# Two-layer hybrid encoder on one core: low parts of the queries two heads to a tile, second logits matmul over 64 rows

## The chip, the cores and the metric

The kernel runs on one core of a Trainium2 chip. The metric is the device time of one execution in microseconds (us). TensorE is called PE below, VectorE DVE, ScalarE ACT, GpSimd POOL; SP issues most DMA transfers.

## What is computed

Two layers of an encoder trunk on 512 tokens of width 1024. Each layer is a half-step FFN, a mixer of three branches, and another half-step FFN. The change lies in the mixer's two attention branches, which share one routine:

```python
# branch A: own chunk + 8 chunks to the left, learned relative bias; branch C: forgetting attention
qf = rms_norm(q, gq) * (dh ** -0.5)          # per head, 8 heads of 64
kf = rms_norm(k, gk)
logits = einsum('qhd,khd->hqk', qf, kf) + bias_or_forget_term      # masked
p = softmax(logits)
out = einsum('hqk,khd->qhd', p, v)
```

All inputs and outputs are f32.

## The kernel before

Matrix products are made from split operands: a number x is held as a rounded part `hi` (fp32r, the type that PE multiplies in one pass) and a rest `lo = x - hi`. A product of two split operands takes three matmuls (`triple`, L119 to L121): hi by hi, lo by hi, hi by lo.

Layout: the hidden state is transposed, features on the 128 partitions, 512 tokens in the columns. The eight heads of 64 are handled as four pairs p; a pair fills 128 partitions.

Queries and keys are projected with tokens on partitions, normalised, and then turned by PE, one pair at a time, into an "mm" bank of PSUM (`turn(p)`, L664). From there they go to blocks [128, 2, 512] of the pool "b", which has 17 blocks:

- Block `b` of a pair has one half for each head (`odd` = 0, 1). Half `odd` holds the head's 64 rows of hi in the rows `own` (0 to 63 for the first head, 64 to 127 for the second). In the rows `other` a key block holds the key's lo part (`low`, L679), and a query block holds the query's hi once more (L676).
- So the first logits matmul (L771), over all 128 rows, gives q_hi k_hi + q_hi k_lo at once.
- The term q_lo k_hi is left. For it each pair of queries has a second block, `lows[p]`: half `odd` has the head's lo in the rows `own` and zeros, written by a memset on POOL (L677), in the rows `other`. The second logits matmul (L772) runs over all 128 rows and adds this product to the same bank; the zeros meet the keys' lo.

`logits(h, i, strips)` makes one row block i (128 queries, (i + 1) x 128 keys) of head h: two matmuls, then DVE adds bias or mask and takes the maximum (L775), ACT the exponential (L779), POOL or, for i = 3, DVE scales (L782). `turn` of the attention transposes the probabilities on PE (L794) and splits them (L798, L799); `weigh` multiplies with the values (L816, L817) and brings the result out (L820, L821). There are 8 heads x 4 blocks in each branch, so 32 pairs of logits matmuls a branch and 128 in all.

Between these steps a filler feeds PE: branch A's attention is filled with the projections of branch C (among them the turning of C's queries once heads 2 and 4 of A are reached), branch C's with products of the merge. The Python code calls steps by delays counted in PE work (`later`, `poll`); the scheduler that builds the program then sets each engine's final order by its own estimate of times, so an edit of one step can move its neighbours.

Of the kernel before, what the change touches and what calls it, by code (L numbers as in the profile page):

```python
# [15 lines left out]
F32 = mybir.dt.float32  # L16
# [6 lines left out]
P = 128  # L23
# [7 lines left out]
HD = 64  # L31
# [9 lines left out]
def encoder_kernel(tc, xT, c, w_ada, b_ada, gains, w_gate, w_up, w_down, w_qkv, w_f, w_ubg,  # L41
                   qk_gain, rel, fbias, w_pool, pool_scale, w_branch, w_out, inv_cnt, w_first, out):
    nc = tc.nc
# [12 lines left out]
    mm = nc.tensor.matmul  # L56
# [7 lines left out]
    def st(shape, dt, tag, bufs):  # L64
        return sb.tile(shape, dt, tag=tag, bufs=bufs, name=nm(tag))
# [4 lines left out]
    def mmt(shape=(P, T)):  # L70
        return ps.tile(list(shape), F32, tag="mm", bufs=4, name=nm("mm"))

    def blk(tag, dt=F32R):
        bufs = {"xv": 4, "v2": 4, "b": NB}[tag]
        return st([P, 2, T], dt, tag, bufs)

    def t1(cols=T):
        return st([P, cols], F32, "t1", 2)

    def t2(cols=T):  # L80
        return st([P, cols], F32, "t2", 3)
# [16 lines left out]
    def later(delay, fn, group=None):  # L98
        t = Task(pe[0] + delay, fn, group)
        tasks.append(t)  # L100
        return t
# [267 lines left out]
    def split_to(hi, lo, src, lo_eng=nc.vector):  # L369
        nc.scalar.copy(hi, src)  # L370
        lo_eng.tensor_tensor(lo, src, hi.bitcast(F32), op=ALU.subtract)  # L371
# [266 lines left out]
    def proj_qk(l, col, gcol, is_q, res, pre=None, norm=None):  # L638
        lows = []
        qs = []  # L640

        def evac(t, a):
            if t == 0:
                qs.extend((st([P, NT, T], F32, "ptb", 2), st([P, NT, H], F32, "qss", 1)))
            qn, ss = qs
            nc.scalar.copy(qn[:, t, :], a)
            sq = t2(T)
            nc.scalar.activation(sq, a, AF.Square)  # L648
            nc.vector.tensor_reduce(ss[:, t, :], sq.rearrange("p (h d) -> p h d", h=H), axis=AX.X, op=ALU.add)

        yield from proj(l, col, evac, pre, norm)
        qn, ss = qs
        v = st([P, NT * H], F32, "nt_v32", 2)
        nc.vector.tensor_scalar(v, ss.rearrange("p t h -> p (t h)"), 1.0 / HD, EPS, op0=ALU.mult, op1=ALU.add)
        r = rsqrt(v, NT * H)
        for t in range(NT):
            q3 = qn[:, t, :].rearrange("p (h d) -> p h d", h=H)
            eng = nc.vector if t % 2 else nc.gpsimd
            eng.tensor_tensor(q3, q3, r[:, t * H:(t + 1) * H].unsqueeze(2).to_broadcast([P, H, HD]), op=ALU.mult)

        def turn(p):
            pt = mmt()
            for t in range(NT):
                nc.tensor.transpose(pt[:, t * P:(t + 1) * P], qn[:, t, p * P:(p + 1) * P], ident)  # L664
            pe[0] += 2.2
            b = blk("b")
            if is_q:
                lows.append(blk("b"))
            first, second = slice(0, HD), slice(HD, P)
            for odd, (own, other) in enumerate(((first, second), (second, first))):  # L670
                dst = b[:, odd, :]
                gc = gcol[own, :]
                nc.scalar.activation(dst[own, :], pt[own, :], AF.Identity, scale=gc)
                low = dst[other, :]
                if is_q:
                    nc.scalar.activation(low, pt[own, :], AF.Identity, scale=gc)  # L676
                    nc.gpsimd.memset(lows[p][other, odd, :].bitcast(F32), 0.0)  # L677
                    low = lows[p][own, odd, :]
                nc.vector.scalar_tensor_tensor(low, pt[own, :], gc, dst[own, :].bitcast(F32),  # L679
                                               op0=ALU.mult, op1=ALU.subtract)  # L680
            res.append((b, lows[p]) if is_q else b)

        todo = [lambda p=p: turn(p) for p in range(4)]
        turns.append(todo)

        def ready(p):
            if len(todo) >= 4 - p:
                if heads[0] < (Q_GATE if is_q else K_GATE)[p]:
                    later(8, lambda: ready(p))
                else:  # L690
                    while len(todo) >= 4 - p:
                        todo.pop(0)()

        for p in range(4):
            later(TURN + 12 * p, lambda p=p: ready(p))
# [6 lines left out]
    def finish_turns(upto=3):  # L702

        for todo in turns:
            while len(todo) >= 4 - upto:
                todo.pop(0)()
# [53 lines left out]
    def attention(qs, ks, vs, strip, ys, filler, budget, group):  # L760


        open_pt = {}

        def logits(h, i, strips):
            p, off = divmod(h, 2)
            (q, ql), k = qs[p], ks[p]
            odd = h % 2
            n = (i + 1) * P
            s = mmt()  # L770
            mm(s[:, :n], q[:, odd, i * P:(i + 1) * P], k[:, odd, :n], start=True, stop=False)  # L771
            mm(s[:, :n], ql[:, odd, i * P:(i + 1) * P], k[:, odd, :n], start=False, stop=True)  # L772
            lg = t1(T)[:, :n]
            mx = st([P, 1], F32, "mx", 4)
            nc.vector.tensor_tensor_reduce(out=lg, in0=s[:, :n], in1=strips[i], scale=-1.0, scalar=BIG,  # L775
                                           op0=ALU.add, op1=ALU.min, accum_out=mx)
            pr = t2(T)[:, :n]
            sm = st([P, 1], F32, "sm", 4)
            nc.scalar.activation(pr, lg, AF.Exp, bias=mx, scale=-1.0, accum_out=sm)  # L779
            rs = st([P, 1], F32, "rs", 4)  # L780
            nc.vector.reciprocal(rs, sm)
            (nc.vector if i == NT - 1 else nc.gpsimd).tensor_scalar(pr, pr, rs, None, op0=ALU.mult)  # L782
            pe[0] += 0.5 * (i + 1.5)
            later(LAG_T, lambda: turn(h, i, pr), group)

        def turn(h, i, pr):
            half, c = divmod(i, 2)
            nj = 2 * half + 2
            if c == 0:
                open_pt[h] = st([P, 2, nj, 256], F32R, "ptb" if half else "pta", 2 if half else 1)  # L790
            pt = open_pt[h]
            tp = mmt()
            for j in range(i + 1):
                nc.tensor.transpose(tp[:, j * P:(j + 1) * P], pr[:, j * P:(j + 1) * P], ident)  # L794
            tv = tp[:, :(i + 1) * P].rearrange("p (j q) -> p j q", q=P)
            dh = pt[:, 0, :i + 1, c * P:(c + 1) * P]
            dl = pt[:, 1, :i + 1, c * P:(c + 1) * P]
            nc.scalar.copy(dh, tv)  # L798
            nc.vector.tensor_tensor(dl, tv, dh.bitcast(F32), op=ALU.subtract)  # L799
            pe[0] += 0.55 * (i + 1)  # L800
            if c == 1:
                later(LAG_V, lambda: weigh(h, half, pt), group)

        def weigh(h, half, pt):
            p, off = divmod(h, 2)
            rows = slice(off * HD, off * HD + HD)
            other = slice(HD - off * HD, 2 * HD - off * HD)
            if off == 0 and half == 0:
                ys.append(blk("b"))
            y = ys[p]  # L810
            o = mmt((P, HALF))
            nj = 2 * half + 2
            for j in range(nj):
                q0 = P if j == nj - 1 else 0
                v2 = vs[j][:, h, :, :].rearrange("p a d -> p (a d)")
                mm(o[:, q0:], v2, pt[:, 0, j, q0:], start=(j == 0), stop=False)  # L816
                mm(o[:, q0:], v2, pt[:, 1, j, q0:], start=False, stop=(j == nj - 1))  # L817
            cols = slice(half * HALF, (half + 1) * HALF)
            yl = t1(T)[:, :HALF]
            nc.scalar.copy(yl[rows, :], o[other, :])  # L820
            nc.vector.tensor_tensor(yl[rows, :], o[rows, :], yl[rows, :], op=ALU.add)  # L821
            split_to(y[rows, 0, cols], y[rows, 1, cols], yl[rows, :], nc.gpsimd)
            pe[0] += 1.0 * nj

        for h in range(H):
            strips = strip(h)
            if group == "c":
                finish_turns(h // 2)
            for i in range(NT):
                logits(h, i, strips)  # L830
                if i == NT - 1:
                    heads[0] = h + 1
                poll()
                goal = pe[0] + budget
                while filler is not None and pe[0] < goal:
                    if next(filler, "end") == "end":
                        filler = None
                poll()
        if filler is not None:
            for _ in filler:  # L840
                pass
# [249 lines left out]
```

## Time and profile before

| what | value |
|---|---|
| median of 3 runs | 2472.27 us (2471.41 to 2472.57) |
| profiled execution, its own time | 2472.68 us |
| span in the profile | 2470.9 us |
| PE busy | 2424.9 us, 98% of the span |
| DVE, ACT, POOL busy | 1328.2, 981.6, 377.3 us |
| attention of A and C, layer 0 | about 459 to 685 us of the span |
| attention of A and C, layer 1 | about 1680 to 1908 us of the span |

The span runs from the first to the last instruction; the execution's own time has 1.8 us more around it. Matmuls are pipelined: a row of the timeline gives a start and a modelled duration, and the spacing of the starts tells what a matmul costs in a stream. L numbers are lines of the kernel before. In the changed kernel L673 and L676 become L674 and L677, L679 and L771 keep their numbers, and what follows L771 stands one line lower (L772 becomes L773, L794 L795).

### The profile page before, as it was taken

Reading aid. Unit: us, or ns where it says so; the run is one execution under the profiler, and the core shown is the slowest. Engines: PE = TensorE matmul, PEld = TensorE weight load, DVE = VectorE, ACT = ScalarE, POOL = GpSimd, SP = SyncE. Lnnn points to the kernel's source line nnn. Section 1 sums busy time; section 2 is a strip of 40 time slices with the busy share of each in tenths; the row PEclk is TensorE's granted clock in tenths of the full one; section 3 lists DMA queues with packets and bytes.
Section 4 is the critical chain, followed back from the end, with each engine's and each line's share of the span. In section 5 each row is a group of like instructions: output and inputs, shape, how many; then the busy total and the mean of one; then the engine's idle time right before and its main releaser. Section 6 shows DMA issues by size and latency. Waiting matters only on the chain. (4 is left out here: it accounts for less than half of the span.)

```text
span 2470.9 us, 31073 instructions
## 1 busy us (share of the span) xinstructions
PE 2424.9 (98%) x11898; PEld 2028.9 (82%) x11898; DVE 1328.2 (54%) x2362; ACT 981.6 (40%) x1634; POOL 377.3 (15%) x439
## 2 busy tenths in 40 slices
PE   7999999999999999999999999999999999999999
PEld 5888888777888898888898888978778888888888
DVE  8655536777643465555365533376766434533332
ACT  5322235676632342222342222366765323422221
POOL 2000012144432200000100000123354322000000
PEclk9999999999999999999999999999999999999999
DMA  7655542323333435565335533333233233233322
GB/s 276 222 194 189 195 136 87 87 72 98 104 97 104 150 101 201 173 209 182 120 118 189 189 118 94 128 92 92 67 108 101 86 119 128 77 94 101 95 94 94
DMA packets 116264, 320.03 MB, mean 130 GB/s; under 512 B 11122, under 2 KB 13298, under 8 KB 116116
## 3 DMA queue, kind: packets, MB, share of 16 engines
q1 hardware_dynamic: 114962, 313.86, 38.8%
q0 software_dynamic: 1152, 4.19, 0.4%
q8 instruction: 93, 1.52, 0.3%
q14 instruction: 55, 0.45, 0.1%
q10 hardware_dynamic: 2, 0.00, 0.0%
HBM read 311.64 MB, written 6.38 MB: 129 GB/s over the span
## 5 line engine op out<-in xcount | busy, mean ns | idle before, releaser
L268 ACT CAST whi<-raw 128x1024 fp32r<-128x1024 f32 (+1 forms) x395 | 412.1, 1046 | 1072.7 <-PE acc L120 398.0
L270 DVE TENSOR_TENSOR wlo<-raw,whi 128x1024 fp32r<-128x1024 f32 x387 | 478.7, 1239 | 527.2 <-ACT whi L268 514.7
L121 PE MATMUL mm<-hhi,wlo 128*128 128x512 f32 x1304 | 507.4, 389 | 0.4 <-DVE wlo L270 0.4
L119 PE MATMUL mm<-hhi,whi 128*128 128x512 f32 x1304 | 507.6, 389 | 0.0
L120 PE MATMUL mm<-hlo,whi 128*128 128x512 f32 x1304 | 507.3, 389 | 0.0
L119 PE MATMUL acc<-b,whi 128*128 128x512 f32 (+1 forms) x960 | 356.3, 371 | 0.0
L120 PE MATMUL acc<-b,whi 128*128 128x512 f32 (+1 forms) x960 | 354.6, 369 | 0.0
L121 PE MATMUL acc<-b,wlo 128*128 128x512 f32 (+1 forms) x960 | 354.5, 369 | 0.0
L121 PEld LDWEIGHTS mm<-hhi,wlo 128*128 128x128 f32 x1304 | 244.8, 188 | 51.8 <-DVE wlo L270 0.9
L120 PEld LDWEIGHTS mm<-hlo,whi 128*128 128x128 f32 x1304 | 244.8, 188 | 50.8
L119 PEld LDWEIGHTS mm<-hhi,whi 128*128 128x128 f32 x1304 | 245.1, 188 | 50.5
L197 DVE CUSTOM_DVE_ANT_0 v<-v,b,badac 128x1024 f32<-128x1024 f32 x144 | 189.6, 1318 | 37.1 <-DMA v<-in_w_ada_dram 36.8
L121 PEld LDWEIGHTS acc<-b,wlo 128*128 128x128 f32 x960 | 181.7, 189 | 29.8
L120 PEld LDWEIGHTS acc<-b,whi 128*128 128x128 f32 x960 | 181.5, 189 | 29.6 <-POOL b L371 0.4
L119 PEld LDWEIGHTS acc<-b,whi 128*128 128x128 f32 x960 | 181.2, 189 | 28.6
L119 PE MATMUL acc<-hhi,whi 128*128 128x512 f32 x480 | 190.7, 399 | 1.7 <-ACT hhi L558 1.7
L120 PE MATMUL acc<-hlo,whi 128*128 128x512 f32 x480 | 188.2, 392 | 0.8 <-DVE hlo L561 0.8
L121 PE MATMUL acc<-hhi,wlo 128*128 128x512 f32 x480 | 188.6, 393 | 0.0
L456 DVE TENSOR_TENSOR t<-mm,t 128x512 f32<-128x512 f32 x86 | 59.5, 692 | 203.4 <-PE mm L121 202.4
L119 PE MATMUL acc<-whi,hhi 128*128 128x512 f32 x336 | 137.8, 411 | 4.1 <-ACT t L648 3.7
L121 PE MATMUL acc<-whi,hlo 128*128 128x512 f32 x336 | 132.1, 393 | 0.0
L120 PE MATMUL acc<-wlo,hhi 128*128 128x512 f32 x336 | 131.7, 392 | 0.0
(233 smaller groups left out, 3348.1 us busy)
## 6 DMA issues: line engine op xcount, KB each, us to landing
v<-in_w_ada_dram SPq DMA_DIRECT2D x144, 512.0 KB, 4.6
raw<-in_w_down_dram SPq DMA_DIRECT2D x88, 512.0 KB, 3.8
raw<-in_w_up_dram SPq DMA_DIRECT2D x82, 512.0 KB, 3.6
raw<-in_w_gate_dram SPq DMA_DIRECT2D x79, 512.0 KB, 3.7
raw<-in_w_ubg_dram SPq DMA_DIRECT2D x56, 512.0 KB, 3.6
raw<-in_w_qkv_dram SPq DMA_DIRECT2D x42, 512.0 KB, 3.8
raw<-in_w_branch_dram SPq DMA_DIRECT2D x24, 512.0 KB, 3.7
raw<-in_w_out_dram SPq DMA_DIRECT2D x16, 512.0 KB, 3.7
```

The lines of the kernel that those rows point to most:

```text
L119: mm(o, lh, rh, start=start, stop=False)
L120: mm(o, lh, rl, start=False, stop=False)
L121: mm(o, ll, rh, start=False, stop=stop)
L197: dot = nc.vector.tensor_tensor_reduce(out=raw, in0=raw, in1=silc[0], scale=1.0, scalar=badac[:, l, j, d:d + 1], op0=ALU.mult, op1=ALU.add ...
L268: nc.scalar.copy(hi, raw)
L270: lo_eng.tensor_tensor(lo, raw, hi.bitcast(F32), op=ALU.subtract)
L456: nc.vector.tensor_tensor(pr, pu, sg, op=ALU.mult)
```

## The change

```diff
@@ proj_qk, turn(p)
             b = blk("b")
             if is_q:
-                lows.append(blk("b"))
+                if p % 2 == 0:
+                    lows.append(blk("b"))
...
                 if is_q:
                     nc.scalar.activation(low, pt[own, :], AF.Identity, scale=gc)
-                    nc.gpsimd.memset(lows[p][other, odd, :].bitcast(F32), 0.0)
-                    low = lows[p][own, odd, :]
+                    low = lows[p // 2][own, p % 2, :]
                 nc.vector.scalar_tensor_tensor(low, pt[own, :], gc, dst[own, :].bitcast(F32),
                                                op0=ALU.mult, op1=ALU.subtract)
-            res.append((b, lows[p]) if is_q else b)
+            res.append((b, lows[p // 2][:, p % 2, :]) if is_q else b)
@@ attention, logits(h, i, strips)
             mm(s[:, :n], q[:, odd, i * P:(i + 1) * P], k[:, odd, :n], start=True, stop=False)
-            mm(s[:, :n], ql[:, odd, i * P:(i + 1) * P], k[:, odd, :n], start=False, stop=True)
+            own = slice(odd * HD, odd * HD + HD)
+            mm(s[:, :n], ql[own, i * P:(i + 1) * P], k[own, odd, :n], start=False, stop=True)
```

The two heads of a pair now put their lo parts into the same 512 columns, one in rows 0 to 63, the other in rows 64 to 127, and two pairs share a block. The memsets are gone (32 in the program). The second logits matmul reads 64 rows of the queries' lo and 64 rows of the keys' hi, and PE is set to a tile of 64 by 128 for it, at row 0 or 64; the first stays at 128 by 128.

No instruction is added. Where the memsets go, the scheduler moves some neighbours. Outside the memsets the order changes in one place of each layer: when the queries of pairs 2 and 3 of branch C are turned (at about 518 us in layer 0). ACT writes eight query rows there, four of each bank. Before, the last four of them and what follows on ACT (`mm_4221` and `mm_4236` are the banks with the two turned pairs, `mm_4254` that of weighted values, `mm_4265` that of transposed probabilities):

```order
L673 ACTIVATE b_4226<-mm_4221,qg_117 64x512
L676 ACTIVATE b_4226<-mm_4221,qg_117 64x512
L673 ACTIVATE b_4241<-mm_4236,qg_117 64x512
L676 ACTIVATE b_4241<-mm_4236,qg_117 64x512
L820 COPY t_791_4259<-mm_4254 64x256
L798 CAST ptb_4264<-mm_4265 128x3x128
```

With the change, ACT at the first of the eight query rows (`mm_4206`, `mm_4219` the turned pairs, `mm_4234` the weighted values):

```order
L648 ACTIVATE t_780_4200<-acc_3902 128x512
L674 ACTIVATE b_4211<-mm_4206,qg_117 64x512
L677 ACTIVATE b_4211<-mm_4206,qg_117 64x512
L821 COPY t_787_4239<-mm_4234 64x256
L674 ACTIVATE b_4224<-mm_4219,qg_117 64x512
L677 ACTIVATE b_4224<-mm_4219,qg_117 64x512
```

The copy of the weighted values stands six query rows earlier; the other six now follow it. On PE at the same place, before (the `acc` matmuls are the filler's projection):

```order
L121 MATMUL acc_3914<-whi_4107,hlo 128x512
L119 MATMUL acc_3914<-whi_4113,hhi 128x512
L120 MATMUL acc_3914<-wlo_4114,hhi 128x512
L771 MATMUL mm_4274<-b_3501,b_3283 128x128
L772 MATMUL mm_4274<-b_3501,b_3284 128x128
L121 MATMUL acc_3914<-whi_4113,hlo 128x512
```

With the change, on PE:

```order
L121 MATMUL acc_3903<-whi_4098,hlo 128x512
L771 MATMUL mm_4254<-b_3491,b_3278 128x128
L773 MATMUL mm_4254<-b_3491,b_3279 128x128
L119 MATMUL acc_3904<-whi_4092,hhi 128x512
L120 MATMUL acc_3904<-wlo_4093,hhi 128x512
L121 MATMUL acc_3904<-whi_4092,hlo 128x512
```

The logits pair of the first query block (128x128) stands eight matmuls of the filler earlier, ahead of the projection's last accumulator (`acc_3904`, before `acc_3914`) and no longer inside it. The transposes of the head before and the next logits pair followed it after three matmuls of the filler, and now follow after six. The SP queue's order is the same as before.

## The prediction

> **What bounds the kernel now.** I read the page's busy times first, then the table by stage, then who TensorE (PE) waits for.
>
> ```profile
> PE 2424.9 (98%) x11898; PEld 2028.9 (82%) x11898; DVE 1328.2 (54%) x2362; ACT 981.6 (40%) x1634; POOL 377.3 (15%) x439
> PEclk9999999999999999999999999999999999999999
> ```
>
> PE is busy for 2424.9 of 2470.9 us at the full granted clock; only 46 us of the span are free of a matmul. So nothing that POOL, ACT or DVE save counts unless PE was waiting for it, and whatever is added to PE counts nearly in full. The change touches the attention of branches A and C in both layers; the table by stage has A and C of layer 0, then of layer 1:
>
> ```profile
> 455.00:575.00 120.00, 112.48 (x579) 89.52 (x578) 88.48 (x218) 85.04 (x182) 41.07 (x50) 1.00 0.25 75
> 575.00:690.00 115.00, 110.27 (x586) 90.24 (x587) 74.16 (x200) 72.85 (x175) 60.80 (x86) 0.99 0.35 108
> 1677.00:1797.00 120.00, 112.22 (x578) 89.33 (x576) 88.61 (x218) 84.93 (x181) 41.09 (x50) 1.00 0.25 75
> 1797.00:1910.00 113.00, 108.16 (x576) 88.37 (x577) 72.28 (x200) 71.71 (x174) 61.06 (x85) 0.98 0.34 106
> ```
>
> The columns are the stretch, its length, then busy time and count of PE, weight load, DVE, ACT and POOL. PE lacks 7.5, 4.7, 7.8 and 4.8 us, together 24.8 us. That is all there is to win in the stages that change, and it can cover little of a cost. The waits over the whole span say whom PE waited for:
>
> ```profile
> PE mm L794 <- POOL t L782: 7.1, 16, 0.7
> ...
> PE mm L771 <- DVE b L679: 1.9, 2, 0.9
> ```
>
> L794 transposes probabilities that POOL has scaled (L782): 7.1 us in 16 waits. L771 is the first logits matmul; twice it waited for L679, the DVE instruction that writes the low part of a query.
>
> **Part 1: 32 memsets leave POOL.** Four pairs of heads, two halves, two query projections, two layers.
>
> ```profile
> L677 POOL MEMSET b<- x32: 518/521/792, 419.1 to 1740.9; 64x512 f32 x32
> ...
> who waited for it (us, times):
> busy tenths in 40 slices 0000000000000000000000000000000000000000
> ```
>
> They are 32 x 0.52 = 16.7 us of POOL's 377.3, and the list of who waited for them is empty. Could they have delayed POOL's scaling, for which PE does wait? The clearest place is just around the memsets of layer 0:
>
> ```profile
> 512.98 0.93 POOL L782 TENSOR_SCALAR t<-t,rs 128x256 f32<-128x256 f32 x1 [4.54 <-DVE rs L781]
> 513.96 0.44 PE L794 MATMUL mm<-ident,t 128*128 128x128 f32 x2 [0.65 <-POOL t L782]
> 517.09 2.47 POOL L677 MEMSET b<- 64x512 f32 x4
> 526.14 1.35 POOL L371 TENSOR_TENSOR b<-t,b 64x256 fp32r<-64x256 f32 x1 [6.49 <-ACT b L370]
> ```
>
> Before the scaling that PE waited 0.65 us for, POOL had been idle 4.54 us; after the longest run of memsets it was idle again for 6.49 us. So the memsets ran in POOL's own gaps. Only branch A's stretch has memsets beside such a scaling, and there the waits are (layer 0)
>
> ```profile
> PE mm L794 <- POOL t L782: 2.4, 5, 0.7
> ```
>
> and as much in layer 1. I take 0; bounds are 0 and 2 x 2.4 = 4.8 us won.
>
> **Part 2: fewer blocks.** A query projection takes two blocks of the pool "b" for its low parts, no longer four; the two pairs of one block are written to different columns. No PE wait in the trace names a block's release, so this is 0 by itself. Its visible effect is the order at the moved place, the turning of pairs 2 and 3 of branch C's queries, once in each layer:
>
> ```profile
> 517.58 0.67 ACT L673 ACTIVATE b<-mm,qg 64x512 fp32r<-64x512 f32 x1
> ...
> 523.19 0.37 ACT L820 COPY t<-mm 64x256 f32<-64x256 f32 x1
> 521.80 0.76 DVE L679 SCALAR_TENSOR_TENSOR b<-mm,qg,b 64x512 fp32r<-64x512 f32 x1 [0.67 <-ACT b L676]
> 523.20 0.76 DVE L679 SCALAR_TENSOR_TENSOR b<-mm,qg,b 64x512 fp32r<-64x512 f32 x1 [0.65 <-ACT b L676]
> 522.70 0.30 PE L771 MATMUL mm<-b,b 128*128 128x128 f32 x1 [0.93 <-DVE b L679]
> 524.11 0.63 PE L794 MATMUL mm<-ident,t 128*128 128x128 f32 x4 [0.24 <-DVE b L679]
> ```
>
> Two of the four "mm" banks hold the turned queries until DVE's third and fourth L679 end (522.56 and 523.96); PE waits 0.93 and 0.24 us for them. Now ACT's copy of the weighted values (L820, now L821) comes after two of the eight query rows, not after all eight, so its bank comes free some 4 us earlier and the first logits get it. But PE also meets that logits pair eight matmuls earlier (8 x 0.23 = 1.8 us), and the transposes and logits behind it then need the banks of the turned queries, which are released no earlier, and 0.4 us later because the copy stands in front. My estimate is three waits of 0.2, 0.5 and 0.7 us in place of 1.17 us, so +0.2 us a layer. I take 0; bounds are -2.3 us (both waits gone in both layers) and +3 us.
>
> **Part 3: the second logits matmul over 64 rows.** There are 128 of them: 2 layers, 2 branches, 8 heads, 4 blocks of queries. None with 64 rows is in the trace.
>
> ```profile
> 469.37 0.48 PE L771 MATMUL mm<-b,b 128*128 128x512 f32 x1
> 469.69 0.40 PE L772 MATMUL mm<-b,b 128*128 128x512 f32 x1
> 469.93 0.39 PE L119 MATMUL acc<-whi,hhi 128*128 128x512 f32 x1
> ```
>
> From the start of L772 to the next start is 0.24 us for 512 columns. I expect no less with 64 rows, since its columns are as many: elsewhere the weights' other side shrinks to 40, and the matmuls still start 0.23 us apart (next fence). If it cost nothing at all, 128 x 0.24 = 30.7 us would go; three quarters of them have fewer columns, so this bound is too generous. I take 0.
>
> The open cost is the change of shape on the array: from 128 rows to 64 and back, twice per pair, 256 changes. The nearest row is the one other shape that this kernel mixes in, the 128x40 weights of the forget gates:
>
> ```profile
> 561.62 0.40 PE L121 MATMUL acc<-whi,hlo 128*128 128x512 f32 x1
> 561.85 0.39 PE L718 MATMUL mm<-hhi,ssum 128*40 128x512 f32 x1
> ...
> 565.55 0.40 PE L719 MATMUL mm<-hlo,ssum 128*40 128x512 f32 x1
> 565.78 0.40 PE L771 MATMUL mm<-b,b 128*128 128x512 f32 x1
> ```
>
> Going in takes 0.23 us from start to start and coming out takes 0.23 us, like any other neighbour: 0.00 extra. The next nearest is a change of kind, from the f32 transposes back to a matmul of rounded f32:
>
> ```profile
> 472.01 0.49 PE L794 MATMUL mm<-ident,t 128*128 128x128 f32 x3
> 472.26 0.48 PE L119 MATMUL acc<-whi,hhi 128*128 128x512 f32 x1
> 472.57 0.40 PE L120 MATMUL acc<-wlo,hhi 128*128 128x512 f32 x1
> 472.81 0.40 PE L121 MATMUL acc<-whi,hlo 128*128 128x512 f32 x1
> ```
>
> There the first spacing is 0.31 instead of 0.23 us: 0.08 extra. A matmul that had to run out first would cost its modelled duration less the spacing, 0.39 - 0.23 = 0.16 us; if the next weights could be loaded only then, their time comes on top:
>
> ```profile
> 459.62 0.19 PEld L772 LDWEIGHTS mm<-b,b 128*128 128x128 f32 x1
> ```
>
> That makes 0.35 us. So 256 changes cost 0, 20, 41 or 90 us by these four rows. I take 0, from the row that also changes the array's shape within one kind of operand; it changes columns, though, not rows, and that doubt is the largest of this forecast.
>
> The Trainium skill speaks against the 0: "TensorEngine Tiling (Array Packing)", Key Properties, says that changing the tiling mode, not just the tile, drains TensorE. By that rule the 128x40 weights should have shown a gap too, if they ran as a mode of their own (its Available Configurations list 128x64), and this trace shows none; but "PSUM — Partial Sum Buffer", in its passage on the zero region, notes in passing that float32r matmuls force all column groups, in which case those rows never changed mode. No row here settles it, and by the rule the sum would be some 41 us higher.
>
> **Sum.** The profiled execution took 2472.68 us, 0.41 above the median of the runs. 2472.7 + 0 (memsets) + 0 (order) + 0 (second matmul) + 0 (256 changes) = 2472.7, or 2472 against the median. The likeliest case's own range is 2468 to 2475: down by both waits of part 2 and half of part 1's bound (2.3 + 2.4), up by part 2's 3.
>
> **Rivals.**
>
> Slower: PE runs out at each change between 128 and 64 rows. For it: 128 rows in flight before 64 is a situation that no row shows, and PE has no slack to cover it. Against: the 0.00 of the 128x40 rows. Price: 256 x 0.16 = 41 us, so 2513; at 0.08 it gives 2492, and with an unhidden weight load 2562. It decides from 4.9 / 256 = 0.02 us a change. The skill's rule on tiling modes is this rival.
>
> Faster: POOL's shorter queue brings the scaled probabilities earlier. For it: 4.8 us of PE waits in branch A name POOL. Against: the 4.54 us of idle POOL ahead of the wait shown. Price: at most 4.8 + 2.3 = 7.1 us, so 2465; a second matmul hidden in part by its neighbours would end at a similar time or lower.
>
> A wait in place of another: the new order at the turned queries costs more than it saves. Price at most +3 us, 2475; a measurement of this kernel can tell about 0.2% (4.9 us) from no change, so this counts as the same.
>
> **How the numbers follow.** No change, 2468 to 2475, with or without the new wait: 0.48. Draining in some form: 0.43, of which 0.31 up to 2513 and 0.12 above it. Faster by more than 4.9 us: 0.09. The predicted time is the likeliest case's, 2472. The range 2466 to 2513 leaves out 0.12 above and some 0.05 below.
>
> **What would show it.** Right: the second logits matmul starts as far behind the first, and the next matmul as far behind it, as before (0.24 us at 512 columns); PE's idle time in the four stretches stays near 25 us in all; POOL's busy time falls by 17 us with the same waits of L794. Wrong: spacings around the 64-row matmuls that grow by 0.08 us or more, PE's count unchanged but each attention stretch longer by 5 us or more; or, on the other side, the waits of L794 for POOL gone.

## The result: 2489.4 us, 0.7% slower

The changed kernel took 2489.41 us (median, 2488.98 to 2489.81), the kernel before 2471.84 us (2470.56 to 2472.57) in the same comparison: a ratio of 1.0072, with a 95% interval of 1.0061 to 1.0083. That is 17.6 us more, inside the stated range and on the side to which 0.43 was given. The forecast of no change was wrong.

The page of the profile after:

```profile
PE 2461.0 (99%) x11898; PEld 2032.8 (82%) x11898; DVE 1328.3 (53%) x2362; ACT 981.3 (39%) x1634; POOL 353.3 (14%) x407
PEclk9999999999999999999999999999999999999999
```

PE has as many instructions as before and is busy 36 us longer, at the same clock. POOL lost its 32 memsets (16.7 us) and is busy 24 us less; none of that shows as a gain here. The table by stage, with A and C of layer 0, then of layer 1 (stretch, length, busy time and count of PE, weight load, DVE, ACT, POOL):

```profile
455.00:578.00 123.00, 122.31 (x580) 91.35 (x578) 88.95 (x218) 85.45 (x183) 36.67 (x43) 1.00 0.25 74
578.00:699.00 121.00, 119.24 (x586) 91.06 (x586) 74.03 (x199) 72.56 (x174) 57.74 (x86) 0.99 0.32 103
1686.00:1808.00 122.00, 121.46 (x577) 90.82 (x576) 88.31 (x217) 84.68 (x180) 36.46 (x42) 1.00 0.24 74
1808.00:1929.00 121.00, 118.82 (x587) 90.42 (x588) 74.28 (x201) 73.12 (x175) 58.91 (x86) 1.00 0.31 99
```

PE now lacks 0.7, 1.8, 0.5 and 2.2 us, 5.2 us in place of 24.8. Its waits in the attention of layer 0 are nearly gone. The three longest before (455 to 700 us), and all that are listed after:

```profile
PE mm L794 <- POOL t L782: 3.5, 8, 0.7
PE mm L771 <- DVE t L821: 2.3, 3, 1.0
PE mm L771 <- DVE ptb L799: 1.4, 1, 1.4
```

```profile
PE mm L771 <- DVE mx L776: 0.5, 1, 0.5
PE mm L771 <- DVE t L822: 0.5, 2, 0.3
PE mm L795 <- POOL t L783: 0.3, 1, 0.3
PE mm L795 <- DVE rs L782: 0.3, 1, 0.3
```

So PE waits less and still ends later. The timeline of PE around one logits pair of 512 columns says why:

```profile
485.66 0.39 PE L771 MATMUL mm<-b,b 128*128 128x512 f32 x1
485.98 0.49 PE L773 MATMUL mm<-b,b 64*128 64x512 f32 x1
486.40 0.50 PE L119 MATMUL acc<-whi,hhi 128*128 128x512 f32 x1
486.74 0.40 PE L120 MATMUL acc<-wlo,hhi 128*128 128x512 f32 x1
486.98 0.40 PE L121 MATMUL acc<-whi,hlo 128*128 128x512 f32 x1
```

From start to start: 0.32 us into the 64-row matmul, 0.42 out of it, 0.34 to the one behind that, and then 0.24 as everywhere. In a stream without changes all of these are 0.23. The weight loads of the same moment, and ahead of them those of a pair of the same width in the kernel before (its two logits matmuls start at 483.58 and 483.81):

```profile
483.35 0.19 PEld L771 LDWEIGHTS mm<-b,b 128*128 128x128 f32 x1
483.58 0.19 PEld L772 LDWEIGHTS mm<-b,b 128*128 128x128 f32 x1
483.81 0.19 PEld L119 LDWEIGHTS acc<-whi,hhi 128*128 128x128 f32 x1
```

```profile
485.43 0.19 PEld L771 LDWEIGHTS mm<-b,b 128*128 128x128 f32 x1
485.98 0.18 PEld L773 LDWEIGHTS mm<-b,b 64*128 64x128 f32 x1 [0.36 <-issue]
486.40 0.19 PEld L119 LDWEIGHTS acc<-whi,hhi 128*128 128x128 f32 x1 [0.24 <-issue]
486.51 0.19 PEld L120 LDWEIGHTS acc<-wlo,hhi 128*128 128x128 f32 x1
```

In the kernel before, the load for the second matmul starts as the first matmul starts. In the changed kernel the load for L773 begins only at 485.98, with its own matmul, after 0.36 us in which the weight path did nothing; the load for L119 waits in the same way. The load behind that one (L120, 486.51) starts 0.11 us after the matmul ahead of it, and not together with it. So across a change of rows the next weights are not loaded ahead in these traces. Whether the load waits for the array or the array for the load, no run separates.

Over all pairs, worked out from the timelines of both kernels (medians of the starts' spacing, us, about 30 pairs of each width; the last column runs from the matmul behind the pair, mostly a filler, to the one after it):

| columns | first to second | second to next | next to its next |
|---|---|---|---|
| 128 | 0.14 to 0.23 | 0.11 to 0.25 | 0.28 to 0.34 |
| 256 | 0.12 to 0.21 | 0.12 to 0.31 | 0.23 to 0.34 |
| 384 | 0.22 to 0.27 | 0.18 to 0.37 | 0.23 to 0.33 |
| 512 | 0.31 to 0.40 | 0.23 to 0.43 | 0.23 to 0.34 |

(At 384 and 512 columns the pair often follows f32 transposes, which lengthens the first spacing in both kernels.) Summed over the 128 pairs without idle time, these three spacings were 75.8 us and are 119.4 us: the changes of rows cost PE 43.6 us, 0.17 us each. About 20 us of this came out of waits that PE no longer has (24.8 - 5.2 us in the four stretches).

### The profile page after: what moved, and what is told of

Same layout as the page of the kernel before. It is cut to its first block, busy times and chain, and to the rows that moved or that the text cites. A ratio compares the mean times of both kernels' runs of the same rounds, so it can differ in the third digit from the quotient of the medians.

```text
span 2487.4 us, 31037 instructions
## 1 busy us (share of the span) xinstructions
PE 2461.0 (99%) x11898; PEld 2032.8 (82%) x11898; DVE 1328.3 (53%) x2362; ACT 981.3 (39%) x1634; POOL 353.3 (14%) x407
## 5 line engine op out<-in xcount | busy, mean ns | idle before, releaser
L119 PE MATMUL mm<-hhi,whi 128*128 128x512 f32 x1304 | 507.6, 389 | 0.0
L120 PE MATMUL mm<-hlo,whi 128*128 128x512 f32 x1304 | 507.3, 389 | 0.0
L119 PE MATMUL acc<-b,whi 128*128 128x512 f32 (+1 forms) x960 | 357.3, 372 | 0.0
L120 PE MATMUL acc<-b,whi 128*128 128x512 f32 (+1 forms) x960 | 353.7, 368 | 0.0
L119 PEld LDWEIGHTS mm<-hhi,whi 128*128 128x128 f32 x1304 | 245.0, 188 | 51.0
L120 PEld LDWEIGHTS mm<-hlo,whi 128*128 128x128 f32 x1304 | 244.8, 188 | 50.6
L119 PEld LDWEIGHTS acc<-b,whi 128*128 128x128 f32 x960 | 181.1, 189 | 30.0 <-issue 0.4
L120 PEld LDWEIGHTS acc<-b,whi 128*128 128x128 f32 x960 | 181.2, 189 | 28.9
L119 PE MATMUL acc<-hhi,whi 128*128 128x512 f32 x480 | 193.7, 405 | 1.7 <-ACT hhi L558 1.7
L120 PE MATMUL acc<-hlo,whi 128*128 128x512 f32 x480 | 188.3, 392 | 0.9 <-DVE hlo L561 0.9
L119 PE MATMUL acc<-whi,hhi 128*128 128x512 f32 x336 | 142.4, 425 | 2.6 <-ACT t L648 2.6
L120 PE MATMUL acc<-wlo,hhi 128*128 128x512 f32 x336 | 131.8, 392 | 0.0
```

The lines of the kernel that those rows point to most:

```text
L119: mm(o, lh, rh, start=start, stop=False)
L120: mm(o, lh, rl, start=False, stop=False)
```

## The experiments

Theory 1: the change of rows on the array costs. Theory 2: the moved order at branch C's queries, or what the missing memsets did to it, costs. Two kernels take the two parts of the change apart; one has exactly the order of the kernel before on PE, ACT and DVE, the other that of the changed kernel.

**The rows alone.**

```diff
 (on the kernel before; own as in the change)
-mm(s[:, :n], ql[:, odd, i * P:(i + 1) * P], k[:, odd, :n], start=False, stop=True)
+mm(s[:, :n], ql[own, odd, i * P:(i + 1) * P], k[own, odd, :n], start=False, stop=True)
```

> The kernel before, with its blocks, zeros and memsets, and only the second logits matmul over the 64 rows of its head; every engine's order is that of before. Theory 1 (the change of rows on the array costs: about 0.34 us a pair, 43.6 us of PE in 128 pairs, some 27 us of them covered by waits of the attention): 2487 to 2491 us, like the changed kernel. Theory 2 (the moved order at branch C's queries, or the missing memsets, cost): 2472 us, like before.

Measured 2494.65 us (2492.57 to 2495.72), ratio 1.0091 (1.0077 to 1.0104). Theory 2 is out, and theory 1 has the sign: the rows alone are 5.2 us dearer than the whole change, above the 2487 to 2491 us that theory 1 gave.

**The packing alone.**

```diff
 (on the changed kernel)
-mm(s[:, :n], ql[own, i * P:(i + 1) * P], k[own, odd, :n], start=False, stop=True)
+mm(s[:, :n], ql[:, i * P:(i + 1) * P], k[:, odd, :n], start=False, stop=True)
```

> The changed kernel with two heads to a tile and no memsets, its order unmoved, but the second logits matmul over all 128 rows; the other head's low part then meets the keys' low part, a term of the size of the one that the split leaves out anyway. Theory 1: 2469 to 2473 us, the spacing of the pair as before, 0.23 to 0.24 us at 512 columns. Theory 2: 2487 us or more.

Measured 2467.57 us (2466.62 to 2469.70), ratio 0.9983 (0.9974 to 0.9992): a little under what was expected, and faster than the kernel before and the changed one. Its pair runs without a gap again:

```profile
483.75 0.39 PE L771 MATMUL mm<-b,b 128*128 128x512 f32 x1
483.97 0.39 PE L772 MATMUL mm<-b,b 128*128 128x512 f32 x1
484.20 0.40 PE L119 MATMUL acc<-whi,hhi 128*128 128x512 f32 x1
```

The four times make a square:

| | with zeros, order of before | two heads to a tile, moved order |
|---|---|---|
| second matmul over 128 rows | 2471.7 | 2467.6 |
| second matmul over 64 rows | 2494.7 | 2489.4 |

The 64 rows cost 22.9 or 21.8 us, the packing wins 4.1 or 5.2 us. Each is nearly the same whichever way the other stands (1.1 us apart), so the change is the sum of a small gain and a larger loss.

**The price without cover.** In the FFN's gate and up products PE hardly ever waits (0.4 us ahead of 3 x 1304 matmuls on the page of the kernel before). There 128 extra matmuls were put ahead of an accumulation, once over 64 rows and once over 128:

```diff
 (on the kernel before, in Ffn.unit, for the first 128 products of 512 columns)
+mm(o, w[0][0:HD, 0, :], hhi[0:HD, 0, :], start=True, stop=True)   # ffn_extra64; the control takes all rows
 for k in ks:
     triple(o[:, cols], w[0][:, k, :], ...)
```

> The kernel before with one more matmul of 64 rows and 512 columns ahead of each of 128 gate or up products of the FFN, where PE never waits; its result is overwritten. Theory 1: each costs its stream of 0.23 us and 0.34 us for the changes of rows, 128 x 0.57 = 73 us, all of it in the time, since no wait covers it: about 2545 us. If a change of rows were dear only beside the logits' own accumulation: 128 x 0.23 = 29 us, 2501 us.

> The control to the one with 64 rows: the same 128 extra matmuls at the same places over all 128 rows. Both theories: 128 x 0.23 = 29 us more than before, 2501 us. What the kernel with 64 rows takes above this one is the whole price of 256 changes without cover: 44 us by theory 1.

Measured 2551.80 us (ratio 1.0322, 1.0308 to 1.0336) and 2502.00 us (1.0121, 1.0106 to 1.0137). The control came out as expected. The 64 rows add 49.8 us, some more than the 44 expected: 0.39 us for each 64-row matmul, 0.195 us a change. The timeline of the kernel with 64 rows has the same 0.39 us, far from any attention: 0.32 - 0.23 into it, 0.43 - 0.23 out of it, 0.33 - 0.23 behind.

```profile
99.96 0.39 PE L122 MATMUL mm<-hhi,wlo 128*128 128x512 f32 x1
100.28 0.50 PE L451 MATMUL mm<-hhi,whi 64*128 64x512 f32 x1
100.71 0.50 PE L120 MATMUL mm<-hhi,whi 128*128 128x512 f32 x1
101.04 0.39 PE L121 MATMUL mm<-hlo,whi 128*128 128x512 f32 x1
101.27 0.39 PE L122 MATMUL mm<-hhi,wlo 128*128 128x512 f32 x1
```

**The change, or the 64 rows themselves?** The 64-row matmul was issued two and three times in a row, ahead of the 128-row one:

```diff
 (on the changed kernel, logits; three64 has the first added line twice)
-mm(s[:, :n], q[:, odd, i * P:(i + 1) * P], k[:, odd, :n], start=True, stop=False)
-mm(s[:, :n], ql[own, i * P:(i + 1) * P], k[own, odd, :n], start=False, stop=True)
+mm(s[:, :n], ql[own, i * P:(i + 1) * P], k[own, odd, :n], start=True, stop=True)
+mm(s[:, :n], ql[own, i * P:(i + 1) * P], k[own, odd, :n], start=True, stop=False)
+mm(s[:, :n], q[:, odd, i * P:(i + 1) * P], k[:, odd, :n], start=False, stop=True)
```

> The changed kernel with the 64-row matmul issued twice in a row ahead of the 128-row one (the first result is overwritten), so that 128 pairs of two 64-row matmuls stand beside each other and the number of changes stays 256. Theory 1 (the change costs): from the first 64-row matmul to the second 0.23 us at 512 columns and 0.12 at 256, the cost sits at the way in and out; 2500 to 2510 us. Rival (a 64-row matmul is dear by itself, whatever stands beside it): 0.40 us or more between the two, 2525 us or more.

Measured 2512.75 us (ratio 1.0167, 1.0153 to 1.0181), and 0.34 us from the first to the second at 512 columns (median, starts). That is neither 0.23 nor 0.40, and the time lies between the two ranges given, so theory 1 was too coarse. The same 0.34 stands between the 128-row matmul and the filler behind it, so I read it as a second half of each change. Three in a row put that to the test:

> The changed kernel with the 64-row matmul issued three times ahead of the 128-row one (the first two results are overwritten). If each change of rows costs 0.09 us ahead of the first matmul after it and 0.11 us behind that one, then at 512 columns the starts follow at 0.32 (into the first), 0.34, 0.23, 0.32 (into the 128-row one) and 0.34 us. If every 64-row matmul drags: 0.34 between all three.

```profile
471.84 0.49 PE L772 MATMUL mm<-b,b 64*128 64x512 f32 x1
472.18 0.39 PE L773 MATMUL mm<-b,b 64*128 64x512 f32 x1
472.41 0.39 PE L774 MATMUL mm<-b,b 64*128 64x512 f32 x1
472.73 0.50 PE L775 MATMUL mm<-b,b 128*128 128x512 f32 x1
473.07 0.39 PE L119 MATMUL acc<-whi,hhi 128*128 128x512 f32 x1
473.30 0.40 PE L120 MATMUL acc<-wlo,hhi 128*128 128x512 f32 x1
```

The starts follow at 0.34, 0.23, 0.32, 0.34 and 0.23 us, and the median into the first, where no f32 transpose stands ahead, is 0.33: all as expected to 0.01 us. (Its time, from a single run, was 2526.66 us.) A 64-row matmul between others of its kind costs what a 128-row one does. The loads agree: behind the first 64-row matmul (471.84) the next load starts 0.11 us later, behind the second (472.18) at once, and the load for the 128-row one only with its own matmul (472.73).

```profile
471.95 0.19 PEld L773 LDWEIGHTS mm<-b,b 64*128 64x128 f32 x1
472.18 0.18 PEld L774 LDWEIGHTS mm<-b,b 64*128 64x128 f32 x1
472.73 0.19 PEld L775 LDWEIGHTS mm<-b,b 128*128 128x128 f32 x1 [0.37 <-issue]
```

Here all 64-row matmuls in a row use the same rows; a step from rows 0 to 63 straight to rows 64 to 127 was not run.

A change costs 0.09 us ahead of the first matmul after it (0.32 - 0.23) and 0.11 us behind that one (0.34 - 0.23), 0.20 us together.

**Are columns dear too?** One more matmul with 64 columns of weights over all rows was put ahead of each pair:

```diff
 (on the kernel before)
+mm(s[:HD, :n], ql[:, odd, i * P:i * P + HD], k[:, odd, :n], start=True, stop=True)
 mm(s[:, :n], q[:, odd, i * P:(i + 1) * P], k[:, odd, :n], start=True, stop=False)
```

> The kernel before with one more matmul ahead of each logits pair that uses 64 columns of weights over all 128 rows (a tile of 128 by 64; its result is overwritten). If any change of the tile's shape costs like the change of rows: 0.32 us into it and 0.42 out of it at 512 columns. If columns are free, as the 128x40 weights of the forget gates seemed to show: 0.23 us in and out.

```profile
484.62 0.40 PE L121 MATMUL acc<-whi,hlo 128*128 128x512 f32 x1
484.86 0.39 PE L771 MATMUL mm<-b,b 128*64 128x512 f32 x1
485.09 0.39 PE L772 MATMUL mm<-b,b 128*128 128x512 f32 x1
485.31 0.39 PE L773 MATMUL mm<-b,b 128*128 128x512 f32 x1
```

It is 0.24 us in and 0.23 out (the time, from a single run, was 2489.11 us). The forget gates' 128x40 rows had been read rightly, but they speak of columns only.

**One branch at a time.** The second matmul over 64 rows in A alone, or in C alone, over 128 in the other:

```diff
 (on the changed kernel)
-own = slice(odd * HD, odd * HD + HD)
+own = slice(odd * HD, odd * HD + HD) if group == "a" else slice(0, P)     # only_c64: "c"
```

> Two heads to a tile, the second logits matmul over 64 rows in branch A alone, over 128 rows in branch C (where the other head's low part meets the keys' low part). If cost follows the number of changes, half of the 21.8 us that all 256 add to the kernel with 128 rows: about 2478 us. If branch A's waits of 10 us covered it all but C's did not: 2470 us.

> The same with 64 rows in branch C alone. If cost follows the number of changes: about 2478 us, and the two halves add up to 21.8 us. If branch C carried the whole: 2486 us or more.

Measured 2476.85 us (ratio 1.0020, 1.0011 to 1.0029) and 2483.38 us (1.0048, 1.0034 to 1.0062): 9.3 and 15.8 us over the packed kernel with 128 rows. Together that is 25.1 us, 3.3 more than the 21.8 of both at once. The split is not even, against the 2478 us expected for each. What the changes cost PE is even: the spacings of a branch grew by some 11 us a layer in either (18.9 to 30.2 in A, 18.7 to 29.8 in C, layer 0). What the waits cover is not: from the packed kernel to these two, PE's idle time fell from 6.3 to 0.6 us in A's stretch (455 to 578 us) and from 4.2 to 2.0 us in C's (578 to 699 us).

**What covers, and where the 4 us come from.** Of some 44 us that the changes of rows cost PE, only 22 reached the time; the rest was covered, that is, it took the place of waits. Two more kernels ask whether the attention covers any added PE work:

```diff
 (on the packed kernel with 128 rows: attn_extra128_packed)
+mm(s, q[:, odd, i * P:(i + 1) * P], k[:, odd, :], start=True, stop=True)
 mm(s[:, :n], q[:, odd, i * P:(i + 1) * P], k[:, odd, :n], start=True, stop=False)
 (fill_extra128, in triple, while attention runs)
+if start and filling[0]:
+    for _ in range(2):
+        mm(o, lh, rh, start=True, stop=True)
```

> The kernel with two heads to a tile and 128 rows, and one more 128-row matmul of 512 columns ahead of each logits pair (overwritten): 128 x 0.23 = 29.4 us more PE work in the attention and no change of rows. If the attention's waits cover added PE work of any kind, as they covered about half of the rows' cost: 2476 to 2482 us. If they do not: 2497 us.

> The kernel with two heads to a tile and 128 rows, and two more 128-row matmuls of 512 columns at the start of each of the 28 accumulations that fill PE in a layer's attention (overwritten), 112 in all: 112 x 0.23 = 25.8 us more PE work, in the filler, not ahead of the logits. If it matters where added PE work stands, and work in the filler gives POOL, ACT and DVE time to end what PE else waits for: at least 10 us are covered, 2478 to 2483 us. If only a fifth is covered wherever it stands, as with the matmuls ahead of the logits: about 2488 us.

Measured 2491.32 us (1.0077, 1.0061 to 1.0093) and 2487.55 us (1.0060, 1.0043 to 1.0076): 23.8 of 29.4 us and 20.0 of 25.8 us reached the time, counted from the packed kernel's 2467.57 us (the kernel before, in the three comparisons, moved by 1.1 us). So about a fifth was covered in either, and not half or the 10 us asked for. The pages say where the difference lies: PE's idle time in the whole span (span less busy time) is 42.7 us in the packed kernel, 37.4 and 42.1 us with plain extra matmuls, and 26.4 us in the changed kernel. In these two kernels the scheduler saw the extra matmuls and moved the order again on PE, ACT and DVE, so waits were spread anew (in the second, PE waits 7.5 us for DVE's L825 alone). The change of rows by itself moved nothing: with 64 and with 128 rows the order is the same. But a moved order alone does not keep the waits open: the kernels with two and three 64-row matmuls have a moved order too, and PE is idle for 26.0 and 27.3 us. It may be that waits shrink only under PE time that the scheduler does not count on; that is argued, not shown. No run here holds the order fixed under plain extra work in the attention, so this stays open.

Two kernels ask for the cause of the packing's 4 us:

```diff
 (on the packed kernel with 128 rows: packed_dummyset)
+nc.gpsimd.memset(zz[other, :], 0.0)          # three times, zz a tile of 128 columns
 (packed_4blocks: one block for each pair, as before; half 0 of each is used)
-if p % 2 == 0:
-    lows.append(blk("b"))
+lows.append(blk("b"))
-low = lows[p // 2][own, p % 2, :]
+low = lows[p][own, 0, :]
-res.append((b, lows[p // 2][:, p % 2, :]) if is_q else b)
+res.append((b, lows[p][:, 0, :]) if is_q else b)
```

> The kernel with two heads to a tile and 128 rows, its order on PE, ACT and DVE unmoved, with 96 memsets of 64x128 to a tile of their own put back on POOL at the turning of the queries, so that POOL has about the work of before. If the 4 us that it wins over before come from the moved order and the freer blocks: 2466 to 2469 us. If they come from POOL's shorter queue: 2471 us or more.

> The kernel with 128 rows and no memsets, but with four blocks for the low parts of a projection, as before; its order is that of the packed kernel on every engine. If the number of blocks is worth nothing: 2466 to 2470 us. If the freer blocks are the 4 us: 2471 us or more.

Measured 2469.16 us (0.9989, 0.9980 to 0.9998) and 2467.98 us (0.9983, 0.9973 to 0.9993). With four blocks the time is that of the packed kernel, so the number of blocks is worth nothing that shows. With POOL's work put back (377.8 us busy, as 377.3 before) it is 1.6 us above the packed kernel by the medians; the intervals overlap, so POOL's share is small and may be nothing. What remains, some 2.5 us, is put down to the moved order by subtraction; no run moves the order alone. The packed kernel's waits in layer 0's attention agree in part: the wait of the logits for the turned queries (L679) fell from 0.9 to 0.3 us, that for POOL from 3.5 to 3.1.

```profile
PE mm L794 <- POOL t L782: 3.1, 7, 0.7
...
PE mm L771 <- DVE b L679: 0.3, 1, 0.3
```

## Why the prediction was wrong, step by step

The bound was read rightly: PE carries the time, and what POOL saved did not count.

*Part 1, memsets at 0:* right within the noise. Work put back on POOL made a difference of 1.6 us by the medians, inside the bounds of 0 to 4.8 us.

*Part 2, blocks at 0, order at 0 with bounds -2.3 and +3 us:* blocks right, order mis-sized. The packing as a whole wins 4.1 us (0.9983, 0.9974 to 0.9992); some 2.5 us of it are left for the order, at the lower bound. Three new waits of 0.2, 0.5 and 0.7 us were estimated for each layer; in layer 0 the packed kernel's logits wait 0.3 us for L679.

*Part 3, the second matmul at 0:* right. Between its own kind a 64-row matmul of 512 columns costs 0.23 us.

*Part 3, the 256 changes at 0:* this is the step that failed. It took the price from the 128x40 rows because they too change the array's shape. A change of columns costs nothing in this kernel, at 40 and at 64 columns; a change of rows costs 0.195 us where nothing covers it (49.8 us for 256 in the FFN), and in the attention 43.6 us of PE time, of which some 22 reached the kernel's time. The doubt was named ("it changes columns, though, not rows") and then not followed. The f32 transposes, with their 0.31 us behind a change of kind, were the nearer relative: a similar spacing, 0.34 us, stands behind every change of rows.

*The rival that drains:* it named the place of the cost, but not how it comes about. Its 41 us are near the 43.6 by luck in part: they come from a matmul that has to run out, 0.16 us ahead of each change, where the traces show 0.09 us ahead of the first matmul and 0.11 us behind it. The load that is no longer hidden, with which the forecast came to 0.35 us a change, was there too, and the whole came to 0.20. Its variant of 0.08 us gave 2492 us, close to the measured time, but with half the price and no cover.

*"Whatever is added to PE counts nearly in full":* wrong for this change. Of some 44 us of PE time 22 reached the kernel's time, so the rival's 2513 us was off by 24 us, more than the forecast by 17. The 24.8 us of idle PE were read in the table and then said to cover little of a cost; 20 us of them went. For plain extra matmuls the sentence is nearer the truth: four fifths of their PE time reached the kernel's time.

That the time falls inside the stated range says little for the sum: the range reached up to 2513 us for the rival's sake.

The 17.6 us measured are then -4.1 (packing) and +21.8 (changes of rows, after cover). That these add up is no further test, since both were taken against the same packed kernel; the test is that both have nearly the same size on the other way round the square (+22.9 and -5.2).

"TensorEngine Tiling (Array Packing)" of the Trainium skill, Key Properties, had the sign: a change of tiling mode drains TensorE. The trace agrees in that a change of rows costs 0.20 us; that the array runs empty it does not show, as the 64-row matmul starts at 485.98, before the modelled end of the one ahead (485.66 + 0.39 = 486.05). For 128x64 and 128x40 weights it shows no cost (0.23 us in and out); that these ran as a mode of their own, no run here shows. "TensorE: Matmul & The Clock Gate" of the Trainium skill, Part 2, says that weight loads are pulled ahead of matmuls in flight when the row groups do not conflict or the load goes to the background weight buffer. In these traces loads are pulled ahead from 128 rows to 128 (483.58 for the matmul at 483.81) and from 64 to 64 (472.18 for the one at 472.41), and not from one to the other.

## What to carry to other kernels

Before a matmul is cut down to the rows that it needs, look at what stands beside it: if the neighbours use other rows, each switch can cost what it cost here, 0.20 us of PE time, while the zeros that it saves cost PE nothing (0.23 us from start to start at 512 columns, over 64 rows or 128). In this kernel the better version keeps the packing and all 128 rows: the other head's low part meets only the keys' low part, a term of the size that the split already leaves out, and no zeros are needed (2467.57 us, 0.9983 of before). And take a price from a row that differs from the new operation in the same respect, rows for rows and columns for columns, or keep the whole span between the bounds open.

## What the runs showed of the hardware that was not expected

A change between 128 and 64 rows of weights costs fp32r matmuls 0.20 us at 512 columns, in two parts: 0.09 us ahead of the first matmul on the other side and 0.11 us behind it, with the weight path idle for 0.24 to 0.37 us. Over 256 changes in the FFN that was 49.8 us. A change between 128 and 64 columns of weights costs nothing (0.24 us in, 0.23 out, as in any stream of these matmuls).
